# One more PSUM bank for a projection, a later chain of compressed tiles, and joint column-tiled runs

## The chip, the cores and the metric

The kernel runs on one core of a Trainium2 chip. A core has TensorE (matrix products, results into the PSUM memory only), VectorE, ScalarE and GpSimd for elementwise work, and SyncE, which here issues the DMA transfers. Each engine runs its own list of instructions in order and waits on semaphores for the others. The kernel divides PSUM into eight tiles of 128 x 512 fp32 values, called banks here. The time is device microseconds of one execution; lower is better.

## The reference

One layer of a hybrid decoder on 512 tokens of 1024 features, in fp32. One input projection of the normed rows feeds three groups of heads, each is multiplied by its own gate, and one output projection is added to the residual:

```
h = rms_norm(x); proj = h @ w_in
y = concat[ NSA(q, kv, gates) * silu(z_n),        # 8 heads, 2 kv groups of 4
            Pool(v_p) * silu(z_p),                # running means over 2, 4, 8, 16 tokens
            MemAttn(q_m, mem) * silu(z_m) ]       # 4 heads over 256 memory tokens
out = x + y @ w_out
```

NSA adds three attentions per head, weighted by gates: over 31 compressed blocks of keys, over selected blocks, and over a window. With 512 tokens the selection and the window take in all earlier tokens, so both are plain causal attentions with keys and values of their own.

## The kernel before

Rows of the sequence are worked in four tiles t of 128 queries. An early stage (to about 100 us) makes keys, values, queries and the compressed blocks. The late stage interleaves two streams and is what the change touches.

The first stream, mixers(), consists of 40 units. Units 0 to 7 are memory attention (two pairs of heads hp, four tiles each), units 8 to 39 are NSA, eight heads for each tile t in the order 0, 1, 2, 3. A unit is a score product into a bank pS, a softmax on VectorE and ScalarE (softmax_pair, lines 594 to 619), a turn (transposes on TensorE into a bank pT, copied by ScalarE into the tiles pt0 and pt1), and after every fourth unit a product with the values into the bank pO, followed by a VectorE multiplication with the gate. in_turn (line 762) writes it so that the turn of a unit comes two units after its scores, and its product one turn later. The product of the probabilities with the values is column-tiled: the weights are 128x64 and the two halves of the output's partitions belong to two heads or groups (lines 747 and 697).

The second stream, tasks(), is filler: the gate projections z_m, z_n (two weight loads), z_p and the pool projection, each as two halves of 24 matmuls (z_group, pool_group), then pool_out, the splits of the products into high and low parts (split_y), and the first output tiles (out_tile). Every gate half accumulates in the one bank pJ (ps_proj) and is read by silu (line 785) on VectorE. A third, short stream is the compressed attention, in two chains of two tiles (compressed_pair): scores and a softmax on VectorE up to line 647, then four transposes (line 652) and a copy (line 655) which give the tiles cs_p that the NSA products need.

The loop from line 1022 on joins them. Each unit gives a credit by SHARE (1.5 for a memory unit, 2.1, 0.9, 0.5 and 0.3 for NSA tiles 0 to 3), each whole credit calls one step of the filler; starts says at which unit a part of a compressed chain is called, each for 1.5 more credit. The order so written is not yet the order on the engines: the kernel is built with schedule_with_timeline_sim (line 1085), which lays out the instructions by a model of their times, with the program's order as priority; only those given to keep_in_program_order (pinned) keep their order among themselves.

PSUM is fully given out: four banks pS, one pJ, one pO, two pT. The tiles pt0 and pt1 have two buffers each; both memory products use pt0.

Of the kernel before, what the change touches and what calls it, by code (L numbers as in the profile page):

```python
# [10 lines left out]
F32 = mybir.dt.float32  # L11
# [9 lines left out]
T = 512  # L21
NT = T // 128
# [3 lines left out]
G = 2  # L26
R = 4
# [68 lines left out]
def layer(ctx: ExitStack, tc: tile.TileContext, x, x_t, mem, mem_t, positions, x_first, w_in, w_cmp1, w_cmp2, cmp_pos,  # L96
          w_pool, w_mem_kv, w_out, cst, out):
    nc = tc.nc
    nc = tc.nc
# [17 lines left out]
    def ps_wide():  # L117
        return pp.tile([128, 512], F32, name="pS", bufs=4)

    def ps_proj():  # L120
        return pp.tile([128, 512], F32, name="pJ", bufs=1)

    def ps_out():
        return pp.tile([128, 512], F32, name="pO", bufs=1)
# [20 lines left out]
    pinned = tc.keep_in_program_order  # L145
# [261 lines left out]
    v_sw = sp.tile([128, NT, 2, 128], F32, name="v_sw")  # L407
    v_cz = sp.tile([128, G, R, HD], F32, name="v_cz")
    gate = sp.tile([128, NT, H, 3], F32, name="gate")
    v_m = sp.tile([128, 2, MEM], F32, name="v_m")  # L410
# [248 lines left out]
    def nsa_scores(t, g, h):  # L659
        n = (t + 1) * 128  # L660
        tq = slice(t * 128, (t + 1) * 128)
        if t < 2:
            pv = ps_wide()[:, 0:2 * n].rearrange("p (b k) -> p b k", b=2)
            for i, kk in enumerate((k_hh, k_ll)):
                nc.tensor.matmul(pv, q_st[:, h, tq], kk[:, :, g, 0:n], start=(i == 0), stop=(i == 1))  # L665
            pv = [pv[:, b] for b in range(2)]
        else:
            pv = [ps_wide()[:, 0:n] for _ in range(2)]
            for b in range(2):
                for i, kk in enumerate((k_hh, k_ll)):  # L670
                    nc.tensor.matmul(pv[b], q_st[:, h, tq], kk[:, b, g, 0:n],  # L671
                                     start=(i == 0), stop=(i == 1))
        return softmax_pair(pv, n, causal[:, T - n:], q_nr[:, t, h:h + 1], gate[:, t, h, 1:3])

    def nsa_turn(pts, t, g, rr, p):
        n = (t + 1) * 128
        for b in range(2):
            pt = ps_t()
            for kt in range(t + 1):
                nc.tensor.transpose(pt[:, kt * 128:kt * 128 + 128], p[:, b, kt * 128:kt * 128 + 128], ident)  # L680
            nc.scalar.activation(pts[b][:, :, g, rr, :],  # L681
                                 pt[:, 0:n].rearrange("p (k q) -> p k q", k=t + 1), AF.Copy)

    def nsa_values(t, rp, pts, pc, o):

        tq = slice(t * 128, (t + 1) * 128)
        calls = []
        for b in (1, 0):
            for kt in range(t + 1):
                for g in (1, 0):  # L690
                    calls.append((o[g * 64:g * 64 + 64, rp * 2:rp * 2 + 2, :], v_sw[:, kt, b, g * 64:g * 64 + 64],
                                  pts[b][:, kt, g]))
        for r in (rp * 2, rp * 2 + 1):
            for g in (1, 0):
                calls.append((o[g * 64:g * 64 + 64, r, :], v_cz[:, g, r, :], pc[:, g, :]))
        for i, (dst, v, p) in enumerate(calls):
            m = nc.tensor.matmul(dst, v, p, start=(rp == 0 and i < 2), stop=(rp == 1 and i >= len(calls) - 2),  # L697
                                 skip_group_check=True)
            tc.keep_in_program_order(m)
        zt = z_n[:, rp * 2:rp * 2 + 2, tq]  # L700
        nc.vector.tensor_mul(zt, o[:, rp * 2:rp * 2 + 2], zt)
        if t == ORDER[3]:
            split_y(zt, rp * 2, 2, tq)

    def nsa_units():

        for t in ORDER:
            held = {}
            for rp in range(2):
                for n, (g, rr) in enumerate(((0, 0), (0, 1), (1, 0), (1, 1))):  # L710
                    def turn(p, t=t, rp=rp, n=n, g=g, rr=rr, held=held):
                        if n == 0:
                            held[rp] = [(lp, right_pool())[b].tile([128, t + 1, G, 2, 128], F32, name=f"pt{b}", bufs=2)
                                        for b in range(2)]
                        nsa_turn(held[rp], t, g, rr, p)

                    def values(t=t, rp=rp, held=held):
                        if rp == 0:
                            held["o"] = ps_out().rearrange("p (r q) -> p r q", r=R)
                        nsa_values(t, rp, held[rp], pcs[t], held["o"])  # L720

                    yield (t, lambda t=t, g=g, rp=rp, rr=rr: nsa_scores(t, g, g * R + rp * 2 + rr), turn,
                           values if n == 3 else None)


    def memory_scores(hp, t):
# [8 lines left out]
    def memory_turn(pm, t, p):  # L735
        pt = ps_t()
        for j in range(2):
            for kt in range(2):
                nc.tensor.transpose(pt[:, (j * 2 + kt) * 128:(j * 2 + kt + 1) * 128],
                                    p[:, j, kt * 128:kt * 128 + 128], ident)  # L740
        nc.scalar.activation(pm[:, :, :, t * 128:(t + 1) * 128], pt.rearrange("p (j k q) -> p j k q", j=2, k=2), AF.Copy)

    def memory_values(hp, pm):
        o = ps_out()
        for kt in range(2):
            for j in range(2):
                pinned(nc.tensor.matmul(o[j * 64:j * 64 + 64, :], v_m[:, kt, (hp * 2 + j) * 64:(hp * 2 + j + 1) * 64],
                                        pm[:, j, kt, :], start=(kt == 0), stop=(kt == 1)))
        nc.vector.tensor_mul(z_m[:, hp], o, z_m[:, hp])

    def memory_units():
        for hp in range(2):
            held = {}
            for t in range(NT):
                def turn(p, t=t, held=held):
                    if t == 0:
                        held["pm"] = lp.tile([128, 2, 2, T], F32, name="pt0", bufs=2)
                    memory_turn(held["pm"], t, p)
                yield ("m", lambda hp=hp, t=t: memory_scores(hp, t), turn,
                       (lambda hp=hp, held=held: memory_values(hp, held["pm"])) if t == NT - 1 else None)  # L760

    def in_turn(units):

        queue, after = [], None
        for kind, scores, turn, values in units:
            queue.append((turn, scores(), values))
            if len(queue) > 2:
                turn, p, values = queue.pop(0)
                turn(p)
                if after:  # L770
                    after()
                after = values
            yield kind
        for turn, p, values in queue:
            turn(p)
            if after:
                after()
            after = values
            yield 3
        after()  # L780


    def silu(dst, ps):
# [2 lines left out]
        nc.scalar.activation(th, dst, AF.Tanh, scale=0.5)  # L786
        nc.vector.scalar_tensor_tensor(dst, th, 1.0, dst, op0=OP.add, op1=OP.mult)

    def z_group(parts, i, dst):
        ps = ps_proj()  # L790
        yield from mm3_steps(ps, col_pairs(parts, i * 128))
        silu(dst, ps)
        yield
# [59 lines left out]
    def split_y(src, c, n, tq, eng=None):  # L853
        nc.scalar.activation(act_hi[:, c:c + n, tq], src, AF.Copy)
        (eng or nc.vector).tensor_sub(act_lo[:, c:c + n, tq], src, act_hi[:, c:c + n, tq].bitcast(F32))
# [123 lines left out]
    def right_pool():  # L979
        if not right:  # L980
            rp_.close()
            right.append(ctx.enter_context(tc.tile_pool(name="probs", bufs=1, side="right", reuse_waits="tile")))
        return right[0]

    def tasks():

        loads = [lambda: chunk(w_in, C_ZM, 256, 4), lambda: zn_parts(0), lambda: zn_parts(1),
                 lambda: chunk(w_in, C_VP, 256, 4), lambda: chunk(w_in, C_ZP, 256, 4),
                 lambda: [out_part(0, 6), out_part(0, 0)]]
        parts = loads[0]()  # L990
        for i, load in enumerate(loads[1:]):
            for r in range(2):
                if r:
                    following = load()
                if i == 3:
                    yield from pool_group(parts, r)
                else:
                    yield from z_group(parts, r, (z_m, z_n, z_n, None, z_p)[i][:, r + 2 * (i == 2)])
            parts = following
        parts += [out_part(0, 2), out_part(0, 4)]  # L1000
        outs.extend(parts)
        for c in range(2):
            yield pool_out(c)
        split_y(z_m, 6, 2, slice(0, T))
        split_y(z_p, 4, 2, slice(0, T))
        for t in ORDER[:3]:
            split_nsa(t)
            yield from out_tile(parts, 0, t, ps_proj)
# [9 lines left out]
    next(fill)  # L1018
    run("rg rq")
    credit = 0.0  # L1020
    starts = {4: "c", 7: "c", 20: "c", 23: "c"}
    for i, kind in enumerate(units):
        credit += SHARE[kind]
        if i in starts:
# [64 lines left out]
```

## Time and profile before

| | |
|---|---|
| median of 3 runs | 286.76 us (286.63 to 288.47) |
| profiled execution | 286.94 us, of which 285.1 from the first to the last instruction |
| granted TensorE clock | 0.998 of 2.4 GHz |
| TensorE busy | 276.4 us (97%) |
| VectorE busy | 203.2 us (71%) |
| ScalarE busy | 167.2 us (59%) |
| chain that ended last | TensorE 91%, VectorE 5%, ScalarE 2%, issue 1% |

Busy time is the union of an engine's instructions. Matmuls overlap each other on TensorE, so the distance from one start to the next says more than a duration. What ended the idle time before an instruction stands behind it in brackets.

### The profile page before, as it was taken

How to read it: one execution, taken by the hardware profiler on the slowest of the kernel's cores; microseconds unless marked ns; L12 is line 12 of the kernel's file. 1: busy time of each engine (PE TensorE's matmuls, PEld its weight loads, DVE VectorE, ACT ScalarE, POOL GpSimd, SP SyncE). 2: the span in 40 equal slices, each digit the busy share in tenths (PEclk: the TensorE clock that was granted, in tenths of full speed). 3: DMA queues.
4: the chain of work that ended last, by engine and by line, in shares of the span. 5: the costliest groups of instructions: out<-in, count | busy, mean ns of one | idle time of the engine just before them, and what ended most of it. 6: DMA issues, size and time to landing. Idle time of an engine off the chain costs nothing.

```text
span 285.1 us, 4709 instructions
## 1 busy us (share of the span) xinstructions
PE 276.4 (97%) x1616; PEld 222.9 (78%) x1616; DVE 203.2 (71%) x609; ACT 167.2 (59%) x397; POOL 20.9 (7%) x57
## 2 busy tenths in 40 slices
PE   8999999999999998999999999998899999999995
PEld 6788899988787786898786878576587778788785
DVE  3659945849368977789958888999896897831122
ACT  4785436775457544484877767837776776734000
POOL 2000190020116000000000000000000000000000
PEclk9999999999999999999999999999999999999999
DMA  7999576553066625014050313604002001100312
GB/s 235 402 387 322 159 183 175 189 178 117 2 182 189 155 87 147 0 28 124 0 147 2 91 57 86 212 5 143 2 1 76 0 1 39 37 0 2 97 51 76
DMA packets 22392, 31.26 MB, mean 110 GB/s; under 512 B 2912, under 2 KB 13024, under 8 KB 22240
## 3 DMA queue, kind: packets, MB, share of 16 engines
q1 hardware_dynamic: 22080, 30.43, 34.4%
q10 hardware_dynamic: 288, 0.52, 0.6%
q8 instruction: 13, 0.21, 0.3%
q14 instruction: 11, 0.09, 0.1%
HBM read 27.84 MB, written 2.10 MB: 105 GB/s over the span
## 4 chain that ended last, share of the span: by engine, by line
PE 91%; DVE 5%; ACT 2%; issue 1%; ACTq 0%
PE pJ L367 9%; PE pJ L368 8%; PE pJ L369 8%; PE pS L901 8%; PE pO L697 7%; PE pT L680 6%; PE pS L357 5%; PE pS L361 5%; PE pS L360 5%; PE pS L369 3%; PE pS L671 3%; PE pS L367 3%; PE pS L368 3%; PE pS L665 2%; PE pO L190 1%; DVE w L601 1%
## 5 line engine op out<-in xcount | busy, mean ns | idle before, releaser
L163 DVE TENSOR_TENSOR wl<-wr,wh 128x1024 fp32r<-128x1024 f32 (+3 forms) x31 | 35.9, 1164 | 16.2 <-ACT wh L160 16.0
L681 ACT ACTIVATE pt<-pT 128x128 f32<-128x128 f32 (+3 forms) x64 | 25.3, 430 | 24.0 <-PE pT L680 24.0
L603 ACT ACTIVATE w<-w,sm_st 128x128 f32<-128x128 f32 (+3 forms) x64 | 35.3, 555 | 5.2 <-DVE sm_st L601 4.7
L160 ACT ACTIVATE wh<-wr 128x1024 fp32r<-128x1024 f32 (+3 forms) x30 | 30.2, 1025 | 13.8 <-PE pO L360 4.0
L601 DVE CUSTOM_DVE_ANT_0 w<-pS,causal,q_nr 128x128 f32<-128x128 f32 (+3 forms) x64 | 32.5, 545 | 5.8 <-PE pT L680 3.3
L367 PE MATMUL pJ<-act_hi,wh 128*128 128x512 f32 x80 | 32.0, 400 | 1.2 <-DVE z_m L785 1.2
L369 PE MATMUL pJ<-act_hi,wl 128*128 128x512 f32 x80 | 31.9, 399 | 0.0
L368 PE MATMUL pJ<-act_lo,wh 128*128 128x512 f32 x80 | 31.6, 395 | 0.0
L680 PE MATMUL pT<-ident,w 128*128 128x128 f32 x160 | 24.8, 276 | 1.2 <-ACT pt L681 0.7
L680 PEld LDWEIGHTS pT<-ident,w 128*128 128x128 f32 x160 | 18.9, 140 | 6.2 <-ACT pt L681 2.1
L618 DVE TENSOR_SCALAR w<-w,sm_st 128x256 f32<-128x256 f32 (+2 forms) x64 | 22.7, 400 | 0.8
L367 PEld LDWEIGHTS pJ<-act_hi,wh 128*128 128x128 f32 x80 | 15.1, 188 | 5.2 <-DVE z_m L785 1.8
L361 PE MATMUL pS<-wh,act_lo 128*128 128x280 f32 (+1 forms) x56 | 19.0, 340 | 0.0
L697 PE MATMUL pO<-pt,v_sw 128*64 128x256 f32 x160 | 19.0, 384 | 0.0
L357 PE MATMUL pS<-wh,act_hi 128*128 128x280 f32 (+1 forms) x56 | 19.0, 339 | 0.0
L360 PE MATMUL pS<-wl,act_hi 128*128 128x280 f32 (+1 forms) x56 | 18.8, 336 | 0.0
L369 PEld LDWEIGHTS pJ<-act_hi,wl 128*128 128x128 f32 x80 | 15.0, 188 | 3.1 <-issue 0.2
L368 PEld LDWEIGHTS pJ<-act_lo,wh 128*128 128x128 f32 x80 | 15.0, 188 | 2.7
L697 PEld LDWEIGHTS pO<-pt,v_sw 128*64 128x64 f32 x160 | 10.8, 137 | 6.2 <-issue 1.5
L671 PE MATMUL pS<-k_hh,q_st 128*128 128x384 f32 (+1 forms) x32 | 13.2, 412 | 1.2 <-DVE sm_st L601 1.2
L368 PE MATMUL pS<-wl,act_hi 128*128 128x512 f32 (+1 forms) x38 | 13.5, 356 | 0.0
L367 PE MATMUL pS<-wh,act_hi 128*128 128x512 f32 (+1 forms) x38 | 13.5, 364 | 0.0
(277 smaller groups left out, 621.0 us busy)
## 6 DMA issues: line engine op xcount, KB each, us to landing
wr<-in_w_in SPq DMA_DIRECT2D x15, 512.0 KB, 4.7
wr<-in_w_in SPq DMA_DIRECT2D x9, 256.0 KB, 3.3
e<-in_x SPq DMA_DIRECT2D x4, 512.0 KB, 8.2
wr<-in_w_mem_kv SPq DMA_DIRECT2D x4, 512.0 KB, 4.2
wr<-in_w_out SPq DMA_DIRECT2D x4, 512.0 KB, 4.1
wr<-in_w_out SPq DMA_DIRECT2D x8, 256.0 KB, 3.9
w<-in_x SPq DMA_DIRECT2D x8, 256.0 KB, 3.4
e<-in_x_t SPq DMA_DIRECT2D x7, 256.0 KB, 7.2
```

Source lines behind the costliest of these rows:

```text
L160: i = nc.scalar.activation(hi, wt, AF.Copy)
L163: (eng or nc.vector).tensor_sub(lo, wt, hi.bitcast(F32))
L357: first = nc.tensor.matmul(ps, sh, mh, start=(i == 0), stop=False)
L360: nc.tensor.matmul(ps, sh, ml, start=False, stop=False)
L361: nc.tensor.matmul(ps, sl, mh, start=False, stop=(i == n - 1))
L367: nc.tensor.matmul(ps, sh, mh, start=(i == 0), stop=False)
L368: nc.tensor.matmul(ps, sh, ml, start=False, stop=False)
L369: nc.tensor.matmul(ps, sl, mh, start=False, stop=(i == n - 1))
L601: nc.vector.tensor_tensor_reduce(p[:, b, :n], ps[b], mask, r, 3e38, OP.add, OP.min, st[:, 0, b:b + 1])
L603: nc.scalar.activation(p[:, b, :n], p[:, b, :n], AF.Exp, bias=st[:, 0, b:b + 1], scale=-1.0, accum_out=st[:, 1, b:b + 1])
L680: nc.tensor.transpose(pt[:, kt * 128:kt * 128 + 128], p[:, b, kt * 128:kt * 128 + 128], ident)
L697: m = nc.tensor.matmul(dst, v, p, start=(rp == 0 and i < 2), stop=(rp == 1 and i >= len(calls) - 2), skip_group_check=True)
```

## The change

Four edits. The second half of the first gate projection (z_m, r = 1) accumulates in pO instead of pJ. The two memory products are issued together, after the last memory unit, into pO and one bank pS, and both VectorE multiplications follow; in_turn calls them ahead of the next unit's turn. NSA tile 0 collects all four heads of a group (heads 0 to 3 in place of pairs) in one pair of tiles pt0 and pt1, and has one product run instead of two, with 512 columns per instruction where there were 256; tiles 1 to 3 keep two runs. The second part of the second compressed chain is called at unit 26 instead of 23. The diff, without renamed variables that change nothing:

```
-    def nsa_values(t, rp, pts, pc, o):
+    def nsa_values(t, heads, pts, pc, o):
...
+        hs = slice(heads[0], heads[-1] + 1)
...
-                    calls.append((o[g * 64:g * 64 + 64, rp * 2:rp * 2 + 2, :], v_sw[:, kt, b, g * 64:g * 64 + 64],
-                                  pts[b][:, kt, g]))
-        for r in (rp * 2, rp * 2 + 1):
+                    calls.append((o[g * 64:g * 64 + 64, hs, :], v_sw[:, kt, b, g * 64:g * 64 + 64], pts[b][:, kt, g]))
+        for r in heads:
...
-            m = nc.tensor.matmul(dst, v, p, start=(rp == 0 and i < 2), stop=(rp == 1 and i >= len(calls) - 2),
...
+            m = nc.tensor.matmul(dst, v, p, start=(heads[0] == 0 and i < 2),
+                                 stop=(heads[-1] == R - 1 and i >= len(calls) - 2), skip_group_check=True)
             tc.keep_in_program_order(m)
-        zt = z_n[:, rp * 2:rp * 2 + 2, tq]
-        nc.vector.tensor_mul(zt, o[:, rp * 2:rp * 2 + 2], zt)
+        zt = z_n[:, hs, tq]
+        nc.vector.tensor_mul(zt, o[:, hs], zt)
...
-            for rp in range(2):
-                for n, (g, rr) in enumerate(((0, 0), (0, 1), (1, 0), (1, 1))):
...
+            runs = ((0, 1), (2, 3)) if t else ((0, 1, 2, 3),)
+            for heads in runs:
+                order = [(g, r) for g in range(G) for r in heads]
+                for n, (g, r) in enumerate(order):
...
-                            held[rp] = [(lp, right_pool())[b].tile([128, t + 1, G, 2, 128], F32, name=f"pt{b}", bufs=2)
-                                        for b in range(2)]
-                        nsa_turn(held[rp], t, g, rr, p)
...
+                            held[heads] = [(lp, right_pool())[b].tile([128, t + 1, G, len(heads), 128], F32,
+                                                                     name=f"pt{b}", bufs=2) for b in range(2)]
+                        nsa_turn(held[heads], t, g, r - heads[0], p)
...
-                    yield (t, lambda t=t, g=g, rp=rp, rr=rr: nsa_scores(t, g, g * R + rp * 2 + rr), turn,
-                           values if n == 3 else None)
+                        nsa_values(t, heads, held[heads], pcs[t], held["o"])
+
+                    yield (t, lambda t=t, g=g, r=r: nsa_scores(t, g, g * R + r), turn,
+                           values if n == len(order) - 1 else None)
...
-    def memory_values(hp, pm):
-        o = ps_out()
...
-        nc.vector.tensor_mul(z_m[:, hp], o, z_m[:, hp])
+    def memory_values(pms):
+
+        os = [ps_out(), ps_wide()]
+        for hp, (o, pm) in enumerate(zip(os, pms)):
...
+        for hp, o in enumerate(os):
+            nc.vector.tensor_mul(z_m[:, hp], o, z_m[:, hp])
...
                 yield ("m", lambda hp=hp, t=t: memory_scores(hp, t), turn,
-                       (lambda hp=hp, held=held: memory_values(hp, held["pm"])) if t == NT - 1 else None)
+                       (lambda: memory_values(pms)) if hp == 1 and t == NT - 1 else None)
...
-            queue.append((turn, scores(), values))
+            queue.append((kind, turn, scores(), values))
             if len(queue) > 2:
-                turn, p, values = queue.pop(0)
+                of, turn, p, values = queue.pop(0)
+                if after and after[0] == "m":
+                    after[1]()
                 turn(p)
-                if after:
-                    after()
-                after = values
+                if after and after[0] != "m":
+                    after[1]()
+                after = values and (of, values)
...
-    def z_group(parts, i, dst):
-        ps = ps_proj()
+    def z_group(parts, i, dst, ps_new=ps_proj):
+        ps = ps_new()
...
-                    yield from z_group(parts, r, (z_m, z_n, z_n, None, z_p)[i][:, r + 2 * (i == 2)])
+                    yield from z_group(parts, r, (z_m, z_n, z_n, None, z_p)[i][:, r + 2 * (i == 2)],
+                                       ps_proj if i or not r else ps_out)
...
-    starts = {4: "c", 7: "c", 20: "c", 23: "c"}
+    starts = {4: "c", 7: "c", 20: "c", 26: "c"}
```

The closing loop of in_turn, over the last two units, is rewritten for the new form of its queue and keeps its order.

## Rows read from the trace of the kernel before

**Rows 1.** Busy time of each engine by stage (window, length, engines, PEclk, DMA share, GB/s)

```profile
100.00:110.00 10.00, 8.76 (x47) 6.95 (x46) 7.38 (x31) 6.24 (x12) 1.28 (x2) 1.00 0.35 111
...
150.00:175.75 25.75, 25.75 (x133) 19.28 (x131) 21.74 (x77) 17.69 (x65) 0.00 (x0) 1.00 0.14 42
...
175.75:201.00 25.25, 22.99 (x139) 16.46 (x137) 25.01 (x80) 16.70 (x49) 0.00 (x0) 1.00 0.43 126
```

**Rows 2.** TensorE in order of time, 101 to 110 us (start, duration, instruction, idle before)

```profile
101.61 0.50 PE L367 MATMUL pJ<-act_hi,wh 128*128 128x512 f32 x1 [0.16 <-DVE z_m L785]
...
109.26 0.50 PE L367 MATMUL pJ<-act_hi,wh 128*128 128x512 f32 x1 [1.07 <-DVE z_m L785]
...
109.59 0.40 PE L368 MATMUL pJ<-act_lo,wh 128*128 128x512 f32 x1
...
109.83 0.39 PE L369 MATMUL pJ<-act_hi,wl 128*128 128x512 f32 x1
```

**Rows 3.** VectorE in order of time, 100 to 111 us

```profile
100.86 0.69 DVE L785 TENSOR_TENSOR z_m<-pJ,rstd_t 128x512 f32<-128x512 f32 x1 [0.41 <-PE pJ L369]
...
108.52 0.68 DVE L785 TENSOR_TENSOR z_m<-pJ,rstd_t 128x512 f32<-128x512 f32 x1
...
109.80 0.69 DVE L810 TENSOR_TENSOR wl<-wr,wh 128x512 fp32r<-128x512 f32 x1
```

**Rows 4.** TensorE in order of time, 130 to 153 us

```profile
130.16 0.60 PE L739 MATMUL pT<-ident,w 128*128 128x128 f32 x4
...
130.52 1.20 PE L732 MATMUL pS<-mk,mq_st 128*128 128x256 f32 x8
...
134.10 0.60 PE L739 MATMUL pT<-ident,w 128*128 128x128 f32 x4
...
134.63 1.94 PE L747 MATMUL pO<-pt,v_m 128*64 128x512 f32 x8
...
136.50 0.50 PE L367 MATMUL pJ<-act_hi,wh 128*128 128x512 f32 x1
...
149.87 0.28 PE L665 MATMUL pS<-k_hh,q_st 128*128 128x256 f32 x1
...
152.75 0.38 PE L665 MATMUL pS<-k_hh,q_st 128*128 128x256 f32 x1
```

**Rows 5.** TensorE's weight loads in order of time, 135 to 136 us

```profile
135.11 0.14 PEld L747 LDWEIGHTS pO<-pt,v_m 128*64 128x64 f32 x2 [0.28 <-issue]
...
135.54 0.14 PEld L747 LDWEIGHTS pO<-pt,v_m 128*64 128x64 f32 x2 [0.29 <-issue]
```

**Rows 6.** TensorE in order of time, 165 to 168 us

```profile
165.78 1.08 PE L697 MATMUL pO<-pt,v_sw 128*64 128x256 f32 x8
...
166.70 0.61 PE L697 MATMUL pO<-cs_p,v_cz 128*64 128x128 f32 x8
...
167.24 0.50 PE L369 MATMUL pJ<-act_hi,wl 128*128 128x512 f32 x1
```

**Rows 7.** TensorE in order of time, 178 to 180 us

```profile
178.78 1.08 PE L697 MATMUL pO<-pt,v_sw 128*64 128x256 f32 x8
```

**Rows 8.** TensorE in order of time, 184 to 202 us

```profile
184.70 0.50 PE L367 MATMUL pJ<-wh,act_hi 128*128 128x512 f32 x1
...
186.68 0.39 PE L369 MATMUL pJ<-wh,act_lo 128*128 128x512 f32 x1
...
196.19 0.39 PE L369 MATMUL pJ<-wh,act_lo 128*128 128x512 f32 x1
...
200.28 0.63 PE L652 MATMUL pT<-ident,cs_s 128*128 128x128 f32 x4 [0.69 <-DVE sm_st L611]
...
201.60 0.71 PE L680 MATMUL pT<-ident,w 128*128 128x128 f32 x4 [0.47 <-ACT cs_p L655]
```

**Rows 9.** VectorE in order of time, 185 to 203 us

```profile
185.31 0.67 DVE L855 TENSOR_TENSOR act_lo<-z_n,act_hi 128x512 fp32r<-128x512 f32 x1
...
202.07 0.62 DVE L601 CUSTOM_DVE_ANT_0 w<-pS,causal,q_nr 128x384 f32<-128x384 f32 x1 [0.88 <-PE pT L680]
```

## What I expect of the time, and why

> **What bounds the kernel now.** I read the busy time by stage first, then the chain of waits, then the order of instructions in each place that the diff touches. TensorE is busy through 25.75 us of 25.75 from 150 to 175.75 us, at a granted clock of 1.00, that is 2.4 GHz; VectorE has 4.0 us to spare there [rows 1]. From 175.75 to 201.00 it is the other way round: VectorE is busy 25.01 of 25.25 us and TensorE idles 2.26 [rows 1]. From 100 to 110 us TensorE idles 1.24 [rows 1]. So a TensorE instruction less is worth its start-to-start distance before 175.75, and in the VectorE stretch only what it lets VectorE start sooner. Matmuls overlap on TensorE: one of 0.40 us starts at 109.59, the next at 109.83, 0.24 later [rows 2]. So I price by distances between starts, and an idle time costs 0.16 more than it shows.
>
> **Second gate projection in bank pO.** Now both halves of z_m and all later groups share the one bank pJ, and each group's first matmul (line 367) waits for the VectorE read (line 785) of the group before. The first wait: 0.16 us idle [rows 2], so 0.32; the read behind it runs from 100.86 to 101.55 [rows 3]. The second: 1.07 idle [rows 2], so 1.23; the read began only at 108.52 [rows 3], after other VectorE work. After the stall the second start comes 0.33 behind the first instead of 0.24, 0.09 more [rows 2]; the same is assumed after the first. With half 1 in pO neither wait has a cause: half 1 has a free bank, and z_n's first group takes pJ, which was read by 101.55. Pool pO has been idle since the early projections and is next wanted by the memory product after 150 us. Sum 0.32 + 1.23 + 2 x 0.09 = **1.73 us** gained, on the path. Next late are the weights of z_n's second half: their last low part ends at 109.80 + 0.69 = 110.49 [rows 3]. The group would start 1.73 earlier, at 107.53, and wants that half 12 matmuls of 0.24 later, at 110.41. Cost 0 to 0.2 (the 0.08 here, more if VectorE's order slips), I take 0.1.
>
> **Memory in one run.** Both products are column-tiled: 128x64 weights into the two halves of the output. Eight instructions go from 134.63 to the next other matmul at 136.50, 1.87 us [rows 4]; their weight loads come in pairs 0.43 apart [rows 5], so four pairs are 1.72 and 0.15 is the way out. On the way in, four transposes take 134.63 - 134.10 = 0.53 to the next start, where before a full-width matmul they take 130.52 - 130.16 = 0.36 [rows 4]: 0.17 more. Two runs become one: 0.15 + 0.17 = **0.32 us** gained. The products and their VectorE multiplications stay the same in number; both multiplications now come behind the joint run. The first product moves from 134.63 to where the second stands, between 149.87 and 152.75 [rows 4]; its result isn't read before the split of z_m, which comes after all gate projections and pool_out (line 1004). One of four score banks pS is taken for the run and two multiplications, some 3.4 + 1.4 = 4.8 us; score pairs of a tile-0 unit start at 149.87 and 152.75 [rows 4], about 3 us apart, so four banks last 12: cost 0, and if that cover went, at most the 1.87 that the second half of the run lasts. The turn that follows needs the pt0 buffer which the joint run frees. In in_turn the run therefore stands ahead of the turn; its copies wait for transposes behind the run anyway: 0.
>
> **First tile in one run.** A run of tile 0 is 0.92 us of N=256 and 0.54 of N=128, 1.46 together [rows 6]; two are 2.92. The joint run has eight instructions of N=512, which is what line 747 has (1.72 by the pairs), and sixteen of N=128: 2 x 0.54 less one way out of 0.15, 0.93. So 2.65, a gain of 0.27, with 0.17 for one way in less: **0.44 us**. One multiplication of 512 columns replaces two of 256. This is bounded above by more: the run at 165.78 [rows 6] leaves the TensorE stage for the VectorE stretch, where the second run already starts at 178.78 [rows 7] and TensorE has 2.26 us to spare [rows 1]. If all of its 1.46 + 0.17 were hidden there the part would be worth 1.63, 1.19 more. From below: the product's end comes 2.65 - 1.46 = 1.19 later behind the same start, VectorE's read is about 0.3 longer, and the first output tile wants the low part of z_n. That split runs from 185.31 to 185.98 [rows 9], and its first user is line 369 at 186.68 [rows 8]: 0.7 us of slack against 1.5. Cost 0 to 0.8; the start moves up with TensorE but VectorE is full, so I take the middle, 0.4.
>
> **Second compressed chain three units later.** TensorE stands 0.69 us before line 652's four transposes and 0.47 before the transposes after them, which want a pT bank back from the copy of line 655 [rows 8]: 1.16 us. Line 652 waits for VectorE, where the chain of the same tiles (lines 634 to 647) is queued among the score work of a full queue. VectorE itself loses 0.88 us right after, waiting for transposes behind these [rows 9]. At unit 26 the chain is long done, and VectorE gets its transposes in time. The stretch is VectorE's, so I take its **0.88 us**, not 1.16. The price of the move: pcs[2] is wanted by tile 2's first product, which is issued at step 30 of the loop, four units behind 26; nothing waits. The credit of 1.5 fill steps moves as well. By SHARE, counted through the loop, fill step 42 (second pool_out) goes from unit 23 to 24, step 43 (the splits of line 853 and the start of the first output tile) from unit 23 to 26, step 44 from 25 to 26. With step 43 goes one DMA on SP's queue, the tile's load of x (line 874); it is wanted only at the end of the tile's 24 matmuls, some 6 us after their start [rows 8]. Steps 1 to 41 and their loads keep their units.
>
> **The sum.** 1.73 + 0.32 + 0.44 + 0.88 = 3.37 gained, 0.1 + 0.4 given back: 2.87. The profiled execution took 286.94 us (span 285.10 and 1.84 around it), 0.18 above the median of 286.76. It would come to 284.07, and the median to **283.9**. Its own range, with both costs at their ends (0 to 1.0) and the chain at 0.88 to 1.16, is 283.1 to 284.4.
>
> A rule speaks against this sum. VectorE is full for the 25 us next to the merged runs and the chain, and leaves 4.0 us idle before them [rows 1]. The Trainium skill, "TensorEngine Tiling (Array Packing)", section PSUM Bottleneck, says that tiling speeds up TensorE but not the reading of PSUM, which can become the limit. By it what only TensorE saves there would be lost, and the time would be the second rival's 285.0; by the rows the stretch moves up as a block, 283.9. The trace agrees with the rule inside the stretch and not before it.
>
> **Rivals.**
> *More is hidden.* The first tile's run vanishes into TensorE's idle time in the VectorE stretch (1.19 more) and neither cost appears (0.5): 283.9 - 1.7 = 282.2. For it: those 2.26 us, and VectorE's 4.0 before the stretch, so it could start earlier. Against: z_n's slack of 0.7.
> *VectorE is the bound.* TensorE arrives earlier but VectorE's queue doesn't drain earlier: the merged runs (0.76) and the chain (0.88) give nothing, only the waits at 100 to 110 do: 286.76 - 1.73 = 285.0. For it: 25.01 of 25.25. Against: VectorE had 4.0 us of idle time just before the stretch [rows 1], so it starts when TensorE lets it.
> *The order comes out otherwise.* The build works out each engine's order from a timeline of its own (line 1085), apart from instructions pinned by hand. What the diff moves shifts what is drawn ahead. The waits in this trace are 0.16 to 1.07 us each; three new ones of the larger sort undo the gain: 286.5.
> *Slower: the first output tiles fall behind the stretch.* From 184.70 to 196.19 TensorE's filler is 30 matmuls of output tiles [rows 8], 6.9 us from 184.70 on at 0.23 to 0.24. It needs z_n of tile 0 complete, which now comes after one late run of all four heads, and step 43 stands three units later in the program. If VectorE takes the longer read (line 701) only after its score work, this filler slides behind 201 us, TensorE idles there and pays the 6.9 in its own stage later: 283.9 + 6.9 = 290.8. It decides once the split of z_n ends after about 201, 15 us later than now. Against it: only 0.8 us of delay are accounted for by rows. That the change doesn't do what it says is not among them: bank, run and index are explicit in the code.
>
> **How the numbers follow.** Forecast 0.48, more hidden 0.17, VectorE the bound 0.18, other order 0.09, output tiles late 0.08. About 1% is what a measurement of this kernel can tell from no change: under 283.89 is faster, over 289.63 slower. The forecast's own range lies on both sides of 283.89; with a little over half of it below (0.26) and the first rival (0.17), faster has 0.43, slower the last rival's 0.08, the same 0.49. The range that leaves out the slower rival and the outer ends: 282.2 to 286.5.
>
> **What would show it.** Right: no idle before line 367 between 100 and 110 us, and the first z_n group starting some 1.7 us earlier; 16 instructions of line 747 in one run of about 3.6 us; tile 0's run once, about 2.65 us, after all its eight units; line 652 without idle before it, near or after 203 us, and the 0.88 us of VectorE idle gone. Wrong: idle before line 369 of the first output tile or before z_n's weights; score matmuls of line 665 waiting for a pS bank after the memory run; the stretch of full VectorE longer than 25.3 us; output tile matmuls missing from it.

## The result, and the profile after

The changed kernel took 290.02 us (median of 12 runs, 288.28 to 291.52), the kernel before 286.98 in the same sessions (12 runs, 286.63 to 288.58): ratio 1.0096, interval 1.0076 to 1.0115. It is about 1% slower; I had forecast 283.9, with 286.5 as the upper end.

The 12 runs fall into three groups by their mean granted clock. Three at 1.000 took 288.28 to 288.38, six at 0.994 took 289.56 to 290.68, three at 0.988 took 291.39 to 291.52. Instructions and order are the same in all, so 288.35 - 286.98 = 1.4 us belong to what the change did to the work, and the other 1.7 of the median go with the clock. The kernel before has a second group as well, but more rarely: beside the experiments below, 10 of its 80 runs had a mean clock of 0.994 and took 288.41 to 288.69 us. The profiled run of the changed kernel is of its slowest group (291.39 us, span 289.6). Two executions, one of experiment e15 (395.88 us) and one of the kernel before (457.26), had mean clocks of 0.656 and 0.56 and are in none of the ratios.

Busy time by stage in the profile after (window, length, then TensorE as PE, its weight loads as PEld, VectorE as DVE, ScalarE as ACT, GpSimd as POOL, granted clock, DMA share, GB/s); it answers to [rows 1]:

```profile
100.00:110.00 10.00, 10.00 (x55) 8.39 (x55) 7.92 (x36) 5.46 (x11) 1.59 (x2) 1.00 0.32 94
110.00:120.00 10.00, 9.65 (x47) 7.85 (x46) 6.12 (x14) 3.56 (x6) 0.11 (x1) 1.00 0.25 73
120.00:130.00 10.00, 8.80 (x50) 7.34 (x49) 8.15 (x22) 4.98 (x15) 0.00 (x0) 1.00 0.36 106
150.00:175.75 25.75, 25.04 (x120) 18.43 (x118) 21.53 (x71) 19.13 (x59) 0.00 (x0) 1.00 0.26 75
175.75:201.00 25.25, 23.33 (x116) 15.98 (x118) 22.66 (x76) 16.11 (x53) 0.00 (x0) 0.86 0.30 88
```

The idle time at 100 to 110 us is gone, as forecast: TensorE is busy for 10.00 us instead of 8.76. But 1.55 us of idle time stand right behind it, from 110 to 130. TensorE in order of time there (start, duration, instruction, idle before; only the lines that the text reads), against [rows 2]:

```profile
107.57 0.39 PE L367 MATMUL pJ<-act_hi,wh 128*128 128x512 f32 x1
...
114.75 0.50 PE L367 MATMUL pJ<-act_hi,wh 128*128 128x512 f32 x1 [0.35 <-DVE z_n L794]
...
119.44 2.07 PE L734 MATMUL pS<-mk,mq_st 128*128 128x256 f32 x16
...
123.63 0.50 PE L367 MATMUL pJ<-act_hi,wh 128*128 128x512 f32 x1 [1.20 <-DVE z_n L794]
```

The wait on pJ is now z_n's: the next group stands before VectorE's read of line 794 (785 in the kernel before; line numbers are each kernel's own). More telling is the line between: the first 16 score matmuls of memory. In the kernel before they stood here, ahead of z_n's second group:

```profile
115.30 2.32 PE L732 MATMUL pS<-mk,mq_st 128*128 128x256 f32 x16
...
117.46 0.39 PE L367 MATMUL pJ<-act_hi,wh 128*128 128x512 f32 x1
```

The first z_n group came 1.7 us earlier than before (107.57 instead of 109.26), and the first scores came 4.1 us later. In the order of instructions 92 projection matmuls of the gate stage now stand ahead of them, 72 before: z_m's two groups and z_n's first, and now 20 of the 24 of z_n's second, which starts at 114.75. The order on each engine is made at build time from the build's own timeline and is then fixed; with a free bank for z_m, z_n's second group was drawn ahead of the scores. VectorE, much of whose work here waits for scores, was busy 6.12 us from 110 to 120, and 7.78 in the kernel before:

```profile
110.00:120.00 10.00, 10.00 (x54) 8.30 (x54) 7.78 (x23) 2.68 (x7) 0.11 (x1) 1.00 0.19 52
```

Its busy time from 94 to 175 us (the window row of each kernel, before first) shows that the delay lasts:

```profile
94.00:175.00 81.00, 79.76 (x423) 63.45 (x422) 67.51 (x219) 50.61 (x144) 1.50 (x4) 1.00 0.27 74
```

```profile
94.00:175.00 81.00, 79.25 (x410) 62.94 (x408) 65.66 (x204) 48.64 (x127) 1.81 (x4) 1.00 0.29 81
```

So 1.85 us of VectorE's work are left over at 175 us, from where VectorE was full in the kernel before, while the projections run out sooner: the last groups start up to 2.9 us earlier (166.3 instead of 169.2). The third group of output matmuls started at 215.9 and now starts at 220.5. What TensorE does in between, in order of time:

```profile
173.44 1.12 PE L858 MATMUL pJ<-pl,wpool 128*128 128x512 f32 x2 [0.21 <-DVE z_p L794]
...
175.90 1.12 PE L858 MATMUL pJ<-pl,wpool 128*128 128x512 f32 x2 [0.66 <-DVE z_p L859]
...
177.84 0.50 PE L665 MATMUL pS<-k_hh,q_st 128*128 128x512 f32 x1 [0.52 <-DVE sm_st L601]
...
179.32 1.08 PE L631 MATMUL pS<-kc_hl,q_st 128*128 128x64 f32 x8 [0.74 <-DVE sm_st L601]
180.23 0.48 PE L367 MATMUL pJ<-wh,act_hi 128*128 128x512 f32 x1
...
180.81 0.63 PE L369 MATMUL pJ<-wh,act_lo 128*128 128x512 f32 x1
...
185.75 2.81 PE L697 MATMUL pO<-pt,v_sw 128*64 128x512 f32 x8
188.39 1.04 PE L697 MATMUL pO<-cs_p,v_cz 128*64 128x128 f32 x16
...
191.24 0.50 PE L367 MATMUL pJ<-wh,act_hi 128*128 128x512 f32 x1
...
192.58 0.50 PE L369 MATMUL pJ<-wh,act_lo 128*128 128x512 f32 x1 [0.25 <-DVE act_lo L864]
```

The waits are VectorE's (lines 601, 794, 859). From 180.81 on the same matmul lasts 0.63 us instead of 0.39 (line 369, [rows 8]): that is the clock. In windows of 1 us:

```profile
179.00:180.00 1.00, 0.68 (x6) 0.69 (x7) 1.00 (x5) 1.00 (x5) 0.00 (x0) 1.00 0.67 164
180.00:181.00 1.00, 1.00 (x7) 0.88 (x7) 0.83 (x6) 1.00 (x3) 0.00 (x0) 0.86 0.39 139
181.00:182.00 1.00, 1.00 (x4) 0.80 (x3) 1.00 (x4) 0.90 (x3) 0.00 (x0) 0.50 0.00 0
186.00:187.00 1.00, 1.00 (x4) 0.29 (x4) 1.00 (x4) 0.47 (x2) 0.00 (x0) 0.50 0.09 16
187.00:188.00 1.00, 1.00 (x6) 0.19 (x4) 1.00 (x7) 1.00 (x5) 0.00 (x0) 0.73 0.24 18
```

The granted clock is 0.50, the lower level of 1.2 GHz, from about 180.8 to 187.5 us. The first output tile, which was filler from 184.70 on [rows 8], gets six matmuls in at 180.23 and is then not seen until 191.24.

The memory products, against [rows 4], and the second chain's transposes, against [rows 8]:

```profile
141.40 1.94 PE L751 MATMUL pO<-pt,v_m 128*64 128x512 f32 x8
...
156.58 1.94 PE L751 MATMUL pS<-pt,v_m 128*64 128x512 f32 x8
...
158.54 0.36 PE L665 MATMUL pS<-k_hh,q_st 128*128 128x256 f32 x1
...
211.43 0.66 PE L652 MATMUL pT<-ident,cs_s 128*128 128x128 f32 x4
```

The two products that were to be one run stand 15 us apart. Between them TensorE runs 48 projection matmuls and no score matmul of tile 0; the scores of tile 0's fourth unit are those at 158.54, right behind the second product. The chain's transposes no longer wait.

### The profile page after: what moved, and what is told of

Same layout as the page of the kernel before. It is cut to its first block, busy times and chain, and to the rows that moved or that the text cites. A ratio compares the mean times of both kernels' runs of the same rounds, so it can differ in the third digit from the quotient of the medians.

```text
span 289.6 us, 4687 instructions
## 1 busy us (share of the span) xinstructions
PE 280.1 (97%) x1608; PEld 224.8 (78%) x1608; DVE 203.6 (70%) x608; ACT 167.1 (58%) x397; POOL 20.9 (7%) x57
## 4 chain that ended last, share of the span: by engine, by line
PE 91%; DVE 5%; ACT 2%; issue 0%; ACTq 0%
PE pJ L367 8%; PE pO L697 8%; PE pJ L369 8%; PE pJ L368 8%; PE pS L910 8%; PE pT L680 6%; PE pS L357 5%; PE pS L361 5%; PE pS L360 5%; PE pS L369 3%; PE pS L367 3%; PE pS L368 3%; PE pS L671 3%; PE pO L190 2%; ACT w L603 2%; PE pS L631 1%
## 5 line engine op out<-in xcount | busy, mean ns | idle before, releaser
L681 ACT ACTIVATE pt<-pT 128x128 f32<-128x128 f32 (+3 forms) x64 | 26.0, 432 | 24.6 <-PE pT L680 24.3
L367 PE MATMUL pJ<-act_hi,wh 128*128 128x512 f32 x72 | 28.8, 399 | 1.5 <-DVE z_n L794 1.5
L368 PE MATMUL pJ<-act_lo,wh 128*128 128x512 f32 x72 | 28.5, 396 | 0.0
L369 PE MATMUL pJ<-act_hi,wl 128*128 128x512 f32 x72 | 28.4, 395 | 0.0
L680 PE MATMUL pT<-ident,w 128*128 128x128 f32 x160 | 26.2, 282 | 0.8 <-ACT pt L681 0.8
L697 PE MATMUL pO<-pt,v_sw 128*64 128x256 f32 (+1 forms) x152 | 19.7, 407 | 0.0
L367 PEld LDWEIGHTS pJ<-act_hi,wh 128*128 128x128 f32 x72 | 13.5, 188 | 5.8 <-DVE z_n L794 2.2
L369 PEld LDWEIGHTS pJ<-act_hi,wl 128*128 128x128 f32 x72 | 13.5, 188 | 2.8
L368 PEld LDWEIGHTS pJ<-act_lo,wh 128*128 128x128 f32 x72 | 13.5, 188 | 2.5
```

The lines of the kernel that those rows point to most:

```text
L367: nc.tensor.matmul(ps, sh, mh, start=(i == 0), stop=False)
L368: nc.tensor.matmul(ps, sh, ml, start=False, stop=False)
L369: nc.tensor.matmul(ps, sl, mh, start=False, stop=(i == n - 1))
L697: m = nc.tensor.matmul(dst, v, p, start=(heads[0] == 0 and i < 2), stop=(heads[-1] == R - 1 and i >= len(calls) - 2), skip_group_check=True)
```

## The experiments

Three theories were set against each other first: A, TensorE's filler is missing at 173 to 188 us because of the tile-0 run and the later chain; B, the wait on pJ has only moved to z_n; C, any edit makes the build order things anew, and this one came out badly. In the diffs only the lines that matter are shown. All ratios are to the kernel before, run on the same chip beside them (its medians there were 286.80 to 287.19).

**The four parts alone.**

```diff
 e1  +  z_group(parts, r, ..., ps_proj if i or not r else ps_out)
 e2  +  memory_values, memory_units and in_turn of the changed kernel
 e3  +  nsa_values and nsa_units of the changed kernel
 e4  -  starts = {4: "c", 7: "c", 20: "c", 23: "c"}
     +  starts = {4: "c", 7: "c", 20: "c", 26: "c"}
```

> The kernel before with nothing but the second z_m half in bank pO. Theory A (the time is lost because TensorE's filler is missing at about 173 to 188 us, by the tile-0 run and the later step 43): this part is harmless and keeps its term, 286.98 - 1.73 = 285.3 us at a granted clock of 1.00. Theory B (the wait only moves from z_m to the next groups that share pJ): z_n's groups wait 1.2 to 1.6 us instead, 286.8 us, less than 0.3 from before. Theory C (the build's own order of the engines comes out otherwise with any edit, and loses by chance): a new idle time of over 1 us somewhere after 150 us, 286 to 289.

> The kernel before with nothing but the memory products issued together (two banks, the changed in_turn). Predicted term -0.32: 286.7 us with 16 instructions in one run. Theory A: the two products stand apart in the executed order, as in the changed kernel, so 0: 287.0 us, within 0.3. Theory C: a loss of 0.5 us or more with new idle times after 150 us.

> The kernel before with nothing but tile 0's heads in one column-tiled run. Predicted term -0.44 + 0.4: 286.9 us. Theory A: this is the main loss: the first output tile's matmuls come after about 190 us instead of 184.7, TensorE idles over 2 us more between 175 and 201 us, and the granted clock is at its lower level in some of it: 288.5 to 290 us. Theory C: any value from 286 to 289 without the output tile late.

> The kernel before with nothing but the second chain's end at unit 26 instead of 23. Predicted term -0.88: 286.1 us. Theory A, if the later step 43 (splits and first output tile) is what takes the filler away: 287.5 to 289 us with the first output tile later than 184.7 by 3 us or more. If the tile-0 run alone does it: 286.1 to 287.0 us.

Measured: bank 291.42 us (ratio 1.0162, 1.0147 to 1.0177), memory 288.36 (1.0056, 1.0040 to 1.0073), tile 0 286.27 (0.9976, 0.9960 to 0.9992), chain 286.30 (0.9985, 0.9970 to 0.9999). Theory A, which I held, is wrong: the two parts it blamed are the two that gain. They are edits too, so theory C doesn't hold for any edit. Theory B's waits, 1.55 us, are too small for 4.6, and behind them, at 150.2 us, the bank alone is still 3 us ahead of the kernel before (the same group starts at 153.2 there). The part that I had as the surest gain, 1.73 us, loses 4.6 by itself (0.0162 x 286.8). In its profile the memory scores' data are written by 114.78 + 0.69 = 115.47, and the scores start at 119.13:

```profile
114.78 0.69 DVE L441 TENSOR_TENSOR mk<-pT,mk 128x512 fp32r<-128x512 f32 x1 [0.37 <-ACT mk L440]
```

```profile
119.13 2.07 PE L732 MATMUL pS<-mk,mq_st 128*128 128x256 f32 x16
```

Counted in the timelines up to 170 us, 233 projection matmuls and 18 score matmuls of tile 0 have run with the bank alone, 219 and 24 in the kernel before. That made theory D, which is C with a place: projections drawn ahead of scores that were ready, so that VectorE's work comes later.

**The order held.** If D is right, the bank does no harm once the scores have their old place. The helper that orders one instruction behind others is in the kernel already.

```diff
 e5  kernel before with the bank edit; e6 the changed kernel; each with
     def mm3_steps(ps, pairs, step=2, hold=()):
...
+            if i == 0:
+                behind(first, hold)
     # z_n's second group: hold = the first 16 matmuls of memory_scores
 e7  kernel before with the tile-0 and chain edits
 e8  e7 with the bank edit and the hold
```

> The bank edit alone, with one more ordering: the first matmul of z_n's second projection group stays behind the first 16 memory score matmuls on TensorE, as it stood in the kernel before. Theory D (the freed bank let 20 projection matmuls be put ahead of the first memory scores, which were ready; all score work came later, and the VectorE stretch with it): the loss of 4.6 us goes, 285.0 to 286.5 us, granted clock 1.00, first score matmuls at about 115.5 us, tile 0's first product at about 166 us instead of 172.42. Theory B (the waits on pJ moved to z_n's groups and cost there): these waits remain, 290 to 291 us. Theory F (the lower granted clock at 190 us is the cause by itself): the clock stays 0.994 and the time over 289.

> The changed kernel with the same ordering added. Theory D: the bank's part of the loss goes and the memory part's 1.5 us stays, the tile-0 run and the chain give their 0.5 to 1.1: 286.5 to 287.5 us. If memory's delay and the bank's are the same delay seen twice: no better than 288. Theory B: 290 us as without it.

> Tile 0's joint run and the later chain together, without the bank and the memory edits. If the two gains (0.5 and 0.5 to 0.9 us by their own runs) lie in different places: 285.6 us, the sum. If both take the same idle time out of the VectorE stretch: 286.2 us, that of one. If the first output tile falls behind the stretch (the prediction's slower rival): over 287.

> The bank, tile 0 and the chain with the ordering of the first memory scores, without the memory edit. Theory D with the bank's gain on the path: 284.0 to 285.0 us, faster than every kernel so far. If the bank's gain is taken back by the scores' own readiness at 115.2 us (a wait of about 1 us at the held matmul): 285.2 to 286.0 us, no better than tile 0 and the chain alone.

Measured: e5 286.78 (0.9984, 0.9963 to 1.0004), e6 291.65 (1.0143, 1.0099 to 1.0186), e7 286.47 (0.9971, 0.9956 to 0.9987), e8 286.47 (0.9979, 0.9960 to 0.9997). One ordering of one matmul takes the bank's 4.6 us away (and with it the lower clock: e5's ten runs are at 0.999 to 1.000): for the bank alone the cause is shown. And the bank gains nothing that is clear of zero: e5's interval takes in 1, and e8 is no faster than e7. Both lie above the ranges I had for them (285.0 to 286.5, 285.2 to 286.0). In e5 TensorE idles 0.69 us before the scores, which is their data's readiness, and stands in front of VectorE again later:

```profile
114.59 2.42 PE L736 MATMUL pS<-mk,mq_st 128*128 128x256 f32 x16 [0.69 <-ACT mk L442]
...
183.87 0.50 PE L367 MATMUL pJ<-wh,act_hi 128*128 128x512 f32 x1 [0.93 <-DVE z_p L855]
...
192.05 0.50 PE L367 MATMUL pJ<-wh,act_hi 128*128 128x512 f32 x1 [0.91 <-DVE w L885]
```

e6 missed its 286.5 to 287.5 us, and is even slower than the changed kernel: with the memory edit in, holding the first scores doesn't help. Memory's scores and three tile-0 units' come early there, but the fourth unit's come after 188 projection matmuls (141 in the kernel before, 168 with the memory edit alone, 192 in the changed kernel). So theory D explains the bank alone; in the changed kernel later scores are late as well, and what holds those back is the next question. e6 and e8 differ by the memory edit alone: on top of the other three parts, with the order held, it costs 4.7 us by the ratios and 5.2 by the medians, three times its 1.6 alone. That isn't only the clock, since e6's one run at 1.000 took 290.50. e7 gives 0.8 where the two parts give 0.7 and 0.4 alone; their sum of 1.1 lies inside its interval (0.4 to 1.3), so whether they take the same idle time isn't shown.

**What the memory edit costs.** Two explanations: its second bank is taken from the four that scores go round (G), or the run stands ahead of the next unit's turn and frees buffer pt0 late (H).

```diff
 e9   kernel before:  o = (ps_out, ps_wide)[hp]()      # second product in pS, apart as before
 e10  memory edit, in_turn as before, first tile-0 unit's pt0 half:
+     held[rp][0] = w2k([128, 1, G, 2, 128])
 e13  kernel before with the changed in_turn only
 e14  memory edit with both products, one behind the other, in pO
```

> The kernel before with one word changed: the second memory product goes to a bank of pool pS instead of pO; both products stay separate and in their places. Theory G (the memory edit lost because its bank is taken from the four that the score matmuls go round, so the next three units' score matmuls come behind the product): 288.0 to 288.6 us as the memory edit alone had, and no score matmul of line 665 for some 10 us before the second product. Theory H (the loss comes from the run standing ahead of the next unit's transposes and from buffer pt0 coming back late): 286.6 to 287.2 us.

> The memory edit alone, but with the first tile-0 unit's buffer taken from another pool, so that the products need not stand ahead of that unit's turn: 16 product instructions follow each other on TensorE. Theory G: the bank still costs its 1.5 us, the one run gives back the predicted 0.32: 287.9 to 288.4 us. Theory H: 286.4 to 286.9 us. The run itself, start to the next other matmul: 3.4 us, against 1.87 for one of the two apart.

> The kernel before with only the changed in_turn: a memory product stands ahead of the next unit's transposes instead of behind them; both products stay apart and in pO. If this place is what costs in the memory edit: 287.6 to 288.4 us. If it is the bank or the late first product: 286.6 to 287.2 us.

> The memory edit with both products, one behind the other, in bank pO, so that no score bank is taken. Theory G (the score bank is the cost): 286.8 to 287.2 us. If place and late first product are the cost: 287.8 to 288.5 us as with the bank in pS.

Measured: e9 287.53 (1.0014, 0.9993 to 1.0036), e10 289.89 (1.0102, 1.0086 to 1.0119), e13 286.84 (0.9996, 0.9984 to 1.0007), e14 287.44 (1.0009, 0.9990 to 1.0027). The place ahead of the turn costs nothing. The bank in pS does what G says to the order: in e9 no score matmul of line 665 runs between 141.10 and 152.37, and then three units' come together, right behind the second product.

```profile
150.50 1.94 PE L747 MATMUL pS<-pt,v_m 128*64 128x512 f32 x8
152.37 0.39 PE L665 MATMUL pS<-k_hh,q_st 128*128 128x256 f32 x1
```

The kernel before has three units' in that time, at 142.33, 143.27 and 149.87. The fourth unit's scores stand right behind the product in pS in every kernel that has one there: at 153.45 in the memory edit alone, at 158.54 in the changed kernel, at 157.05 in e6. In e14, with both products in pO, they run at 142.83. So what holds the later scores back in the changed kernel is, by the order, the second product in pS, and there that product itself comes 5 us later than in the memory edit alone (156.58 instead of 151.50). What this makes of the time was not isolated.

For the memory edit alone, e9 costs 0.4 us and e14 0.3, neither clear of zero and both between the two ranges expected of them; the whole edit costs 1.6. Neither explanation alone gives that; whether the two together do is left open. The products stay apart in e14 too (140.96 and 151.54). e10 (289.89) missed both its ranges, 286.4 to 286.9 and 287.9 to 288.4 us: it also changes where a tile-0 buffer lies, which may cost by itself, so its time decides nothing. But it shows the joint run itself:

```profile
151.54 1.94 PE L751 MATMUL pO<-pt,v_m 128*64 128x512 f32 x8
153.31 1.89 PE L751 MATMUL pS<-pt,v_m 128*64 128x512 f32 x8
155.13 0.38 PE L665 MATMUL pS<-k_hh,q_st 128*128 128x256 f32 x1
```

It lasts 155.13 - 151.54 = 3.59 us against 2 x 1.87 for two: the way out of 0.15 is saved, as costed; the way in was not measured.

**The clock and the bound.** e11 and e15 add matmuls whose results are overwritten, in the bank edit's waits; e12 and e16 take work from VectorE.

```diff
 e11  e1, after tile 0's second product:
+     spare.append(ps_out())
+     for _ in range(8):
+         nc.tensor.matmul(spare[0], q_st[:, 0, 0:128], q_st[:, 1, :], start=True, stop=True)
...
 e15  e11, and the same 4 times into po ahead of each matmul of pool_out
 e12  e7 with   split_y(z_p, 4, 2, slice(0, T), nc.gpsimd)
 e16  e8 with the same
```

> The bank edit alone with 8 more matmuls of N=512 (their result is overwritten), which TensorE runs in the idle time of 1.62 us ahead of the first output tile; the order is the same otherwise. Theory K (the granted clock falls to 1.2 GHz because TensorE stands idle there): the clock is 1.00 and the 1.6 us of it come back, less some 0.2 to 0.4 for the extra matmuls: 289.8 to 290.3 us. Theory L (the clock falls for the sparse work of the whole 175 to 190 us, or for no reason in this kernel's order): 0.992 to 0.994 as without them, 291.4 to 292.0 us.

> The bank edit with 16 extra matmuls whose results are overwritten: 8 ahead of the first output tile as before and 4 in front of each of the two pool_out matmuls at 175 to 181 us. If sparse TensorE work from 175 us on brings the lower clock: the granted clock is 1.00 in all runs, and the time 290.0 to 291.0 us, since the score work is late all the same. If the clock falls for another reason: 0.992 to 0.994, 291 to 292 us.

> Tile 0 and the chain, with one of VectorE's subtractions of the stretch from 176 to 201 us (the low part of z_p, 1.23 us, line 857) moved to GpSimd, which is idle there. If VectorE's work sets the length of that stretch (25.25 of 25.25 us busy): 285.2 to 285.6 us against 286.3 without it. If TensorE's or the output tile's dependences set it: 286.1 to 286.5 us; over 286.5 if GpSimd's slower subtraction comes too late for the first output tile.

> Bank, tile 0 and chain with the held order, and the low part of z_p on GpSimd. If VectorE's stretch hides what the bank saves on TensorE, VectorE still does after losing 1.23 us: 285.4 to 285.9 us, the same as without the bank edit (285.67). If the relief brings the bank's gain to the path: 284.0 to 285.0 us.

Measured: e11 290.74 (1.0137, 1.0122 to 1.0152), e15 289.49 (median of its three runs at 1.00; 1.0087, 1.0071 to 1.0104), e12 285.67 (0.9955, 0.9940 to 0.9970), e16 286.47 (0.9980, 0.9968 to 0.9992). Only e12 is within 0.1 us of a range expected of it; e11 lies between its two, e15 0.5 us under its own and e16 0.6 over. The bank alone ran at 0.992 to 0.994 in all its four runs. There the clock fell in the one idle time of 1.62 us ahead of the first output tile, at about 190.3 us. Theory K says that this idle time brings the fall. With eight matmuls in it, three of e11's four runs were still at 0.992 or 0.993, and in the profiled one the fall came at 182.5, 7 us before the filled place. The 1 us rows of the bank alone, then of e11:

```profile
190.00:191.00 1.00, 0.55 (x1) 0.50 (x2) 1.00 (x7) 1.00 (x4) 0.00 (x0) 0.66 0.57 127
```

```profile
182.00:183.00 1.00, 1.00 (x5) 0.82 (x5) 1.00 (x6) 0.95 (x2) 0.00 (x0) 0.76 0.18 70
190.00:191.00 1.00, 1.00 (x6) 0.82 (x5) 1.00 (x8) 1.00 (x5) 0.00 (x0) 1.00 0.84 248
```

So that idle time isn't needed for the fall. Sixteen matmuls over the whole stretch from 175 us gave 1.00 in all three runs and 1.9 us back, although they are work added; the remaining 2.5 us (0.0087 x 287.2) would be what the bank's order costs at the full clock. Sparse TensorE work over the stretch is thus the better explanation of the lower clock, but with three runs it is not proved, and one run speaks against pricing the clock alone: e11's fourth ran at 1.00 and took 291.18 us, the longest of the four. The Trainium skill, "TensorE: Matmul & The Clock Gate", section HAM oscillation — how this bites in real kernels, says that waits between bursts of matmuls throw TensorE back to the lower clock. These runs agree in part only: its example is a long wait in every round of a loop, and here no single wait in the changed kernel between 173 us and the fall is over 0.74 us.

In e12 one VectorE subtraction of 1.23 us runs on GpSimd instead:

```profile
185.82 2.83 POOL L857 TENSOR_TENSOR act_lo<-z_p,act_hi 128x1024 fp32r<-128x1024 f32 x1 [38.84 <-ACT act_hi L856]
```

It takes 2.83 us there, and the kernel is faster than e7 by 0.5 us (the ratios, and the profiled spans of 284.4 and 283.9) to 0.8 (the medians), about half of what VectorE was spared. The intervals of the two ratios overlap, but the slowest of e12's four runs (285.74) is below the fastest of e7's ten (286.05). In e7's order the stretch is VectorE's. e12 is the fastest version, 1.3 us under the kernel before. With the bank edit added, held in order (e16), 0.7 to 0.8 us are lost again. And against e8, which is e16 without GpSimd, the same relief gives nothing (0.9980 and 0.9979). So it didn't bring the bank's gain to the path either, and what bounds the held order was not found.

## Why the prediction was wrong

The step that failed is the one that lets the gains be added up: "by the rows the stretch moves up as a block". It takes a fixed order on each engine that slides forward when a wait goes. The order did not stay: 92 projection matmuls instead of 72 stand ahead of the first memory scores, which come 4.1 us later. And with the order held (e5, e8) the end still did not move clearly. That VectorE's work sets it there is likely, since VectorE is busy 24.51 of the 25.25 us from 175.75 in e5, but e16 does not bear it out.

- *Second z_m half in pO, 1.73 gained.* The waits went as described (8.76 to 10.00 us busy). Their worth is not told from 0: e5 is 0.5 us under the kernel before, with an interval from 0.1 lost to 1.1 gained, and e8 equals e7. Unheld, the edit costs 4.6. I priced a TensorE wait before 175.75 as time on the path because TensorE was busy through 25.75 of 25.75 us; but the projections it is busy with have room behind them, and the scores haven't: in e1 the projections ran 3 us ahead at 150 us, and the kernel lost.
- *Memory, 0.32 gained.* The way out was sized rightly (0.15 measured), but the products did not come together: pinning keeps their sequence, and other work was put between them. The bank's "cost 0", resting on score pairs 3 us apart and four banks lasting 12, was wrong: two more units' scores stand between, at 142.33 and 143.27, 0.94 apart, and with the bank taken three units' came behind the product. Alone the part costs 1.6, on top of the other three with the order held 4.7 to 5.2.
- *Tile 0, 0.44 gained and 0.4 given back.* The joint run takes 181.05 - 178.31 = 2.74 us at full clock in e7 (lines below), 2.65 predicted. The cost did not appear: the part alone gives 0.7, and the first output tile starts at 184.8 us in e3, against 184.70 [rows 8].
- *Chain, 0.88 gained.* 0.4 alone (0.0 to 0.9); the transposes wait no longer, in e4 at 206.16 us.
- *Rivals.* "The order comes out otherwise" is what happened. It had 0.09 and three waits' worth; a changed order moves whole stages of VectorE's work, here 1.4 us at the full clock, and made the lower clock, which I had not considered, the rule instead of the exception: 1.7 more. "VectorE is the bound" is right on the stretch in e7's order (e12) but gave the bank its whole 1.73. The slower rival's first signs are there (output tile matmuls missing from 182 to 191 us), but not by its mechanism: e3 and e4, its two causes, gain.

The joint run of tile 0 in e7:

```profile
178.31 1.94 PE L697 MATMUL pO<-pt,v_sw 128*64 128x512 f32 x8
...
181.05 0.66 PE L680 MATMUL pT<-ident,w 128*128 128x128 f32 x4
```

What stays open: 4.6 and 1.6 lost and 0.8 gained would make 5.4, and the changed kernel loses 3.0, or 1.4 at the full clock; and with the first scores held (e6) it loses more, not less. The parts don't add. With the first scores held, the loss hangs on the memory edit beside the other parts (e6 against e8), by the order through the scores behind its second product; the bank and the memory edit without the other two were not run; which of the late scores makes the changed kernel's 1.4 us was not isolated.

VectorE's busy time from 94 to 175 us goes with the time in most kernels, though it was read only afterwards (clock not taken out): 67.33 us in e7 (286.47), 67.08 in e5 (286.78), 65.96 in e9 (287.53), 65.78 in e2 (288.36), 65.13 in e10 (289.89), 65.06 in e1 (291.42), 64.58 in e6 (291.65). Out of line are e14, 65.75 (287.44), and the changed kernel, 65.66 (290.02, or 288.35 at the full clock). It is a sign and not a proof.

## What to carry to other kernels

Where a build orders instructions by its own timeline, price the removal of a wait twice: what the wait costs, and what is drawn into its place; then look which engine's work comes later. A wait on a busy engine can be worth nothing if the stage behind it belongs to another engine: here taking away 1.24 us of TensorE's idle time gave no clear gain, and one subtraction less on VectorE gave 0.5 to 0.8 in one order of instructions, and nothing in another. When an edit loses, hold the old order with one dependency before judging the edit itself.

## What the hardware did that I had not expected

One kernel in one order has three times, 288.3, about 290 and 291.4 us, which go with the mean granted clock: 1.000, 0.994 and 0.988. In the profiled run of the last group TensorE is at 1.2 GHz for 6.7 us after sparse work. And a subtraction of 128x1024 on GpSimd, 2.83 us against VectorE's 1.23, was still the better place in e7's order, where VectorE is full; in e8's it gained nothing.
